# Hybrid decoder layer: projections of p in eight PSUM banks, splits queued behind evictions, first weight chunk over two queues

## Chip, cores and metric

The kernel runs on one core of one Trainium2 chip. The metric is the device time of one execution in microseconds (us); three executions before the change took 839.36, 839.38 and 839.81 us, median 839.38 us.

## The reference

One layer of a decoder trunk on 256 tokens and 2048 features, all in float32:

```python
h = rmsnorm(x, norm_mix_g)
u = h @ w_in                       # 2048 x 12288: ten fields, split by columns
...                                # short convolution branch yA, gated recurrence branch yB
m = sigmoid(ga) * (yA @ w_a_out) + sigmoid(gb) * (yB @ w_b_out)
x = x + m @ w_o
gate = sigmoid(rmsnorm(x, ple_norm_g) @ w_ple_gate)
x = x + gate * (p @ w_ple_proj)    # p: 256 tokens x 256, w_ple_proj: 256 x 2048
return rmsnorm(x, final_norm_g)
```

The product `p @ w_ple_proj` depends on no other part, and the kernel computes it first. Its result is needed only at the end.

## The kernel before

**Chunks and positions.** All weights are one stream of chunks. A chunk holds 256 rows by 512 columns of a weight matrix as a tile of 128 partitions x 1024 elements (512 KB). Its place in the stream is its position. Positions 0 to 3 are `w_ple_proj`, one chunk for each of its four column groups (kind `PP`); positions 4 to 11 are the first column group of `w_in` (kind `f`), whose left factor is x, transposed and scaled by a gain (`hT`); the rest of `w_in` and the other matrices follow. In this text w4 is the chunk of position 4.

**Three products for one.** [...] `split(pos)` makes the parts of a chunk: ScalarE writes `whi` (L124), then VectorE writes `wlo` (L125), which needs `whi`. `put_x(k)` does the same for the k-th block of 128 features of x (`xh` on ScalarE, L187, and `xl` on VectorE, L188); two blocks are needed for each of the positions 4 to 11. Each position is 12 matmuls of 128x128 by 128x512: two blocks of rows, two halves of the tokens, three products.

**The order of work.** The main loop goes through the positions. Before the matmuls of a position it splits the chunk three positions ahead (`ahead`, with the features of x that belong to it), so four split chunks exist at a time. After them it starts loads of raw chunks (three buffers of two chunks each) and advances the epilogues of earlier groups. The tile layer then orders each engine's instructions and puts in the semaphores. [...]

**PSUM.** `bank(tag)` takes a bank of 128 x 512 from one of two rings of four: `"g"` for the sums of the main loop, two banks for a group (one for each half of the tokens), and `"s"` for small products of the recurrence, which starts later; one `"s"` bank takes the ten matmuls that warm TensorE up. The four groups `PP` take two `"g"` banks each, so the third group reuses the banks of the first.

**The epilogue of `PP`.** `ep_pp` copies the two banks to SBUF on ScalarE (two `ACTIVATE` of 128x512, L643: the eviction) and two steps later sends the tile of 512 KB to DRAM (`kept`, L647), from where it is read back near the end.

**Loads at the start.** The halves of w0 (256 KB each) go over ScalarE's DMA queue (q10), all else over SyncE's (q1), in this order: p transposed (`praw`, 256 KB), w1, the small parameters, w2, then x in eight pieces of 256 KB (`xraw`, piece c for the feature blocks 2c and 2c+1) with w3, w4 and w5 in between, and all eight pieces of x before the first `kept`. Eight semaphores go round among the DMAs, so an issue may also wait for the landing of the one eight before it.

Of the kernel before, what the change touches and what calls it, by code (L numbers as in the profile page):

```python
# [11 lines left out]
AF = mybir.ActivationFunctionType  # L12
# [5 lines left out]
NT = T // P  # L18
D = 2048
KT = D // P  # L20
# [3 lines left out]
CW = 512  # L24
# [20 lines left out]
def hybrid_kernel(ctx, tc, xT, x, pT, prm, gfin, masks, w_in, w_a, w_b, w_o, w_pg, w_pp, out):  # L45
    nc = tc.nc
# [11 lines left out]
    def open_pool(name, side):  # L58
        closers[name] = ExitStack()
        pools[name] = closers[name].enter_context(  # L60
            tc.tile_pool(name=name, bufs=1, side=side, reuse_waits="tile")
        )

    def close_pool(name):
        closers.pop(name).close()
        del pools[name]
# [3 lines left out]
    state = {"tmp": "tmp1"}  # L70
# [3 lines left out]
    def nm(s):  # L74
        uid[0] += 1
        return f"{s}_{uid[0]}"

    def t4(tag="t4", bufs=None):
        bufs = bufs or {"tmp1": 8, "tmp2": 5, "tmp3": 5}[state["tmp"]]
        return pools[state["tmp"]].tile([P, 1024], F32, tag=tag, bufs=bufs, name=nm(tag))  # L80

    def bank(tag):
        return ps.tile([P, CW], F32, tag=tag, bufs=4, name=nm(tag))
# [10 lines left out]
    def load(pos):  # L94
        w, g, c = stream[pos]
        if pos // 2 not in loaded:
            raw = wp.tile([P, 2, 2 * CW], F32, tag="raw", bufs=3, name=nm("raw"))
            loaded[pos // 2] = raw
            if FIRST <= pos < FIRST + 4:
                for i in range(2):  # L100
                    nc.sync.dma_start(out=raw[:, i, :], in_=w[g, :, c + i, :])
            elif pos >= FIRST:
                nc.sync.dma_start(out=raw, in_=w[g, :, c : c + 2, :])
        return loaded[pos // 2]

    def load_first(pos, eng, pieces):

        w, g, c = stream[pos]
        for i in range(pieces):
            s = slice(i * (2 * CW // pieces), (i + 1) * (2 * CW // pieces))  # L110
            eng.dma_start(out=load(pos)[:, pos % 2, s], in_=w[g, :, c, s])  # L111

    def split(pos, halves=(0, 1)):
        w, g, c = stream[pos]
        src = load(pos)[:, pos % 2, :]

        pool, n = (pools["late"], 6) if (pos - state.get("late", len(steps))) % 10 < 6 and "late" in state else (wp, 4)
        if pos not in parts:
            parts[pos] = tuple(
                pool.tile([P, 2 * CW], F32R, tag=tag, bufs=n, name=nm(tag)) for tag in ("whi", "wlo")  # L120
            )
        hi, lo = parts[pos]
        s = slice(halves[0] * CW, (halves[-1] + 1) * CW)
        a = nc.scalar.activation(out=hi[:, s], in_=src[:, s], func=AF.Copy)  # L124
        v = nc.vector.tensor_tensor(  # L125
            out=lo[:, s], in0=src[:, s], in1=hi[:, s].bitcast(F32), op=ALU.subtract
        )
        state["splits"] = (a.ins, v.ins)
# [21 lines left out]
    TOKENS, NORM = 8, 12  # L150
    FIRST = 6

    load_first(0, nc.scalar, 2)
    praw = t4()[:, : 2 * T]
    nc.sync.dma_start(out=praw.rearrange("p (k t) -> p k t", k=2), in_=pT)
    load_first(1, nc.sync, 1)
    prm_t = const.tile([P, PRM_N], F32, name="prm_t")
    nc.sync.dma_start(out=prm_t, in_=prm)

# [480 lines left out]
    def ep_pp(j, psum):  # L640
        pw, d = t4(), dram.tile([P, 1024], F32, tag="kept", bufs=4, name=nm("kept"))
        for t in range(NT):
            nc.scalar.activation(out=pw[:, t * CW : (t + 1) * CW], in_=psum[t], func=AF.Copy)  # L643
        state["kept", j] = d
        yield
        yield
        nc.sync.dma_start(out=d, in_=pw)  # L647
# [73 lines left out]

    state["pT"] = tuple(z[:, :2, :] for z in state["yaT"])
    xraw = [t4() for _ in range(4)]
    for c in range(KT // 2):
        if c + 2 < FIRST:
            load_first(c + 2, nc.sync, 1)
        n = 2 * (c % 2)
        nc.sync.dma_start(
            out=xraw[c // 2].rearrange("p (k t) -> p k t", k=4)[:, n : n + 2, :],
            in_=xT[:, 2 * c : 2 * c + 2, :],  # L730
        )


    warm = pools["tmp1"].tile([P, 4, P], F32, tag="both", bufs=1, name="warm")
# [6 lines left out]
    def put_x(k):  # L741
        put(state["hT"], k, xraw[k // 4][:, (k % 4) * T : (k % 4 + 1) * T], gain(PRM_GMIX, k))
# [10 lines left out]
    def add_squares(q):  # L753

        tc.keep_in_program_order(nc.scalar.activation(
            out=xtok[q], in_=xtok[q], func=AF.Square, accum_out=state["ss1"][:, q : q + 1]
        ))

    def norm_of_x():
        tot = sc(NT, "tot1", 1)  # L760
        nc.vector.tensor_reduce(
            out=tot, in_=state["ss1"].rearrange("p (t h) -> p t h", t=NT),
            axis=mybir.AxisListType.X, op=ALU.add,
        )
        r = state["rstd1"] = rsqrt_of(tot, NT, D, "r1")
        state["rstd1_2"] = sc(NT, "r1s", 1)
        nc.vector.tensor_tensor(out=state["rstd1_2"], in0=r, in1=r, op=ALU.mult)
# [39 lines left out]
    def put_p(k):  # L807

        hi, lo = (z[:, k, :] for z in state["pT"])
        src = praw[:, k * T : (k + 1) * T]  # L810
        nc.vector.tensor_copy(out=hi, in_=src)
        nc.vector.tensor_tensor(out=lo, in0=src, in1=hi.bitcast(F32), op=ALU.subtract)
# [29 lines left out]
    def advance():  # L842
        for e in list(active):
            step(e)

    def finish():
        while active:
            advance()

    def ahead(pos):  # L850

        return LEAD + min(max(pos - (last_group - 20), 0) // 4, 5)
# [8 lines left out]
    psum = None  # L861
    for pos, (gi, c) in enumerate(steps[:last_group]):
        kind, j, w, g, opname = groups[gi]
        nch = w.shape[2]
        if kind == "PG" and j == 0 and c == 0:
            close_pool("m")
            open_pool("late", "left")
            state["late"] = done
        while done < min(pos + 1 + ahead(pos), len(steps)):
            if done == 0:  # L870
                for i in range(2):
                    put_p(i)
                    split(done, (i,))
            else:
                for k in range(2 * (done - 4), min(2 * (done - 4) + 2, KT)) if done >= 4 else ():
                    put_x(k)
                split(done)
            done += 1
        if pos == 4:
            begin()  # L880
        if 0 <= pos - NORM < 4:
            add_squares(pos - NORM)
        if pos == NORM + 3:
            norm_of_x()
        if pos == NORM + 4:
            active.append(ep_f(0, waiting))
            step(active[-1])
            nc.sync.dma_start(out=mask_t, in_=masks)
        if c == 0:
            psum = [bank("g") for _ in range(NT)]  # L890
        hi, lo = parts.pop(pos)
        for i in range(2):
            k = 2 * c + i
            s = slice(i * CW, (i + 1) * CW)
            for n in ((0,), (2,), (1,)) if pos == 0 and i == 0 else ((0, 1, 2),):
                for t in range(NT):
                    product(psum[t], state[opname], k, t, hi[:, s], lo[:, s], k == 0, k == 2 * nch - 1, n)


        if kind == "PG" and j == 0 and c < 2:  # L900
            advance()
        for q in range(done, min(done + AHEAD, len(steps)) if pos >= FIRST else 0):
            load(q)
        if 0 <= pos - TOKENS < 4:
            load_tokens(pos - TOKENS)
        if kind != "PG" or j or c >= 2:
            advance()
        if kind == "O" and j == 0 and c == nch - 3:
            finish()
            third_part()  # L910
        if kind == "O" and j > 0 and c == 1:
            residual(j)
        if kind == "O" and j == 2 and c == 4:
            load_gfin()
        if kind == "PG" and c == 4:
            load_projection(j)
            if j == 2:
                load_projection(3)
        if c == nch - 1:
            if kind == "f" and j == 0:  # L920

                waiting = psum
            if kind == "ga" and j == 0:
                finish()
                second_part()
            if kind == "O" and j == 0:
                state["x1T"] = operand(big, "x", KT)
            if kind == "f" and j == 0:
                continue
            active.append(epilogues[kind](j, psum))  # L930
            step(active[-1])
# [4 lines left out]
    for t, halves in ((0, (0, 1)), (1, (0,)), (1, (1,))):  # L936
        bk, n = bank("g"), CW // 2
        for c in range(nlast):
# [4 lines left out]
            for i in range(2):  # L943
                k = 2 * c + i
                s = slice(i * CW + halves[0] * n, i * CW + (halves[-1] + 1) * n)
# [83 lines left out]
```

## Time and profile before

| what | value |
|---|---|
| median of three executions | 839.38 us |
| the profiled execution, its whole time | 840.28 us |
| its span, first to last instruction | 838.5 us |
| mean granted TensorE clock | 0.993 |
| PE busy | 823.8 us (98%) |
| ScalarE (ACT) busy | 434.8 us (52%) |
| VectorE (DVE) busy | 530.5 us (63%) |
| DMA, mean over the span | 223 GB/s |

PE is TensorE's matmuls, PEld its weight loads, ACT is ScalarE, DVE VectorE, POOL GpSimd, SP SyncE. An L with a number is a line of the kernel. "idle before <-releaser" is the time for which the engine stood still before an instruction, and what ended that. In tables by stretch, PEclk is the clock that the throttle granted to TensorE, as a share of full speed, and the DMA share is the mean busy share of the 16 DMA engines. A matmul's shown duration overlaps with the next one; the distance of starts tells the pace.

### The profile page before, as it was taken

Reading aid. Unit: us, or ns where it says so; the run is one execution under the profiler, and the core shown is the slowest. Engines: PE = TensorE matmul, PEld = TensorE weight load, DVE = VectorE, ACT = ScalarE, POOL = GpSimd, SP = SyncE. Lnnn points to the kernel's source line nnn. Section 1 sums busy time; section 2 is a strip of 40 time slices with the busy share of each in tenths; the row PEclk is TensorE's granted clock in tenths of the full one; section 3 lists DMA queues with packets and bytes.
Section 4 is the critical chain, followed back from the end, with each engine's and each line's share of the span. In section 5 each row is a group of like instructions: output and inputs, shape, how many; then the busy total and the mean of one; then the engine's idle time right before and its main releaser. Section 6 shows DMA issues by size and latency. Waiting matters only on the chain.

```text
span 838.5 us, 9821 instructions
## 1 busy us (share of the span) xinstructions
PE 823.8 (98%) x3754; PEld 684.2 (82%) x3754; DVE 530.5 (63%) x602; ACT 434.8 (52%) x561; POOL 92.3 (11%) x76
## 2 busy tenths in 40 slices
PE   7999999999999999999999999999999999999995
PEld 4888888888888888888888888888888888888885
DVE  6546677787767478696745545645645556669722
ACT  7567465454565465355544444444444455566523
POOL 1000024320000025210000100100100100001210
PEclk8999999999999999999999999999999999999998
DMA  8978555545877554645755755755755687887702
GB/s 308 386 274 303 187 194 194 183 174 190 283 238 245 199 201 157 233 139 196 280 201 200 245 188 186 240 195 201 242 202 188 229 294 273 288 304 287 301 1 101
DMA packets 40656, 187.20 MB, mean 223 GB/s; under 512 B 4640, under 2 KB 13856, under 8 KB 22432
## 3 DMA queue, kind: packets, MB, share of 16 engines
q1 hardware_dynamic: 40032, 185.52, 63.7%
q10 hardware_dynamic: 576, 1.05, 0.3%
q8 instruction: 29, 0.48, 0.2%
q14 instruction: 19, 0.16, 0.1%
HBM read 172.92 MB, written 13.63 MB: 222 GB/s over the span
## 4 chain that ended last, share of the span: by engine, by line
PE 96%; issue 1%; DMA 1%; ACT 1%; DVE 0%; SPq 0%; POOLq 0%; POOL 0%; ACTq 0%
PE g L859 93%; PE s L359 1%; DMA raw<-in_w_pp 1%; PE s L468 0%; ACT whi L124 0%; PE s L480 0%; PE s L481 0%; PE s L479 0%; ACT xs L696 0%; DVE wlo L125 0%; ACT t L679 0%; SPq L111 0%; ACT xh L187 0%; DVE t L675 0%; POOLq L1024 0%
## 5 line engine op out<-in xcount | busy, mean ns | idle before, releaser
L125 DVE TENSOR_TENSOR wlo<-raw,whi 128x1024 fp32r<-128x1024 f32 (+1 forms) x293 | 361.4, 1237 | 263.4 <-ACT whi L124 261.8
L124 ACT ACTIVATE whi<-raw 128x1024 fp32r<-128x1024 f32 (+1 forms) x293 | 308.5, 1057 | 350.8 <-PE g L859 302.3
L859 PE MATMUL g<-whi,xh 128*128 128x512 f32 (+1 forms) x912 | 352.3, 387 | 0.0
L859 PE MATMUL g<-wlo,xh 128*128 128x512 f32 (+1 forms) x912 | 351.5, 385 | 0.0
L859 PE MATMUL g<-whi,xl 128*128 128x512 f32 (+1 forms) x912 | 351.4, 385 | 0.0
L859 PEld LDWEIGHTS g<-whi,xl 128*128 128x128 f32 x912 | 171.3, 188 | 34.4
L859 PEld LDWEIGHTS g<-whi,xh 128*128 128x128 f32 x912 | 171.4, 188 | 33.7
L859 PEld LDWEIGHTS g<-wlo,xh 128*128 128x128 f32 x912 | 171.4, 188 | 33.7
L859 PE MATMUL g<-wlo,mh 128*128 128x512 f32 x128 | 49.6, 389 | 0.0
L859 PE MATMUL g<-whi,ml 128*128 128x512 f32 x128 | 49.5, 389 | 0.0
L859 PE MATMUL g<-whi,mh 128*128 128x512 f32 x128 | 49.5, 389 | 0.0
L604 POOL TENSOR_TENSOR t<-ga,gb 128x512 f32<-128x512 f32 x8 | 14.2, 1795 | 249.0 <-DVE gb L600 249.0
L859 PE MATMUL g<-whi,yaTh 128*128 128x512 f32 x80 | 32.3, 406 | 4.8 <-ACT t L643 4.1
L859 PE MATMUL g<-wlo,yaTh 128*128 128x512 f32 x80 | 32.1, 403 | 0.2 <-DVE wlo L125 0.2
L859 PE MATMUL g<-whi,yaTl 128*128 128x512 f32 x80 | 31.7, 398 | 0.0
L859 PEld LDWEIGHTS g<-wlo,mh 128*128 128x128 f32 x128 | 24.0, 188 | 5.0
L859 PEld LDWEIGHTS g<-whi,ml 128*128 128x128 f32 x128 | 24.0, 188 | 5.0
L859 PEld LDWEIGHTS g<-whi,mh 128*128 128x128 f32 x128 | 24.0, 188 | 4.9
L405 POOL TENSOR_TENSOR t<-b 128x512 f32<-128x512 f32 x10 | 20.9, 2086 | 65.1 <-DVE b L309 33.6
L387 POOL TENSOR_TENSOR X<-t,kT 128x256 f32<-128x256 f32 x12 | 14.1, 1175 | 105.1 <-ACT t L401 63.4
L859 PE MATMUL g<-whi,ybTh 128*128 128x512 f32 x64 | 24.9, 389 | 0.0
L859 PE MATMUL g<-wlo,ybTh 128*128 128x512 f32 x64 | 24.9, 389 | 0.0
(142 smaller groups left out, 539.9 us busy)
## 6 DMA issues: line engine op xcount, KB each, us to landing
raw<-in_w_in SPq DMA_DIRECT2D x93, 1024.0 KB, 4.8
raw<-in_w_o SPq DMA_DIRECT2D x16, 1024.0 KB, 6.7
raw<-in_w_pg SPq DMA_DIRECT2D x16, 1024.0 KB, 5.0
turn<-t SPq DMA_DIRECT2D x72, 128.0 KB, 2.6
t<-turn SPq DMA_DIRECT2D x18, 512.0 KB, 5.3
raw<-in_w_a SPq DMA_DIRECT2D x8, 1024.0 KB, 5.0
raw<-in_w_b SPq DMA_DIRECT2D x8, 1024.0 KB, 5.0
raw<-in_w_in SPq DMA_DIRECT2D x6, 512.0 KB, 6.5
```

Of the source, the lines that this page charges most:

```text
L124: a = nc.scalar.activation(out=hi[:, s], in_=src[:, s], func=AF.Copy)
L125: v = nc.vector.tensor_tensor(out=lo[:, s], in0=src[:, s], in1=hi[:, s].bitcast(F32), op=ALU.subtract)
L359: nc.tensor.matmul(bk[:, s], X[:, 0, h, :], X[:, 1, h, :], start=True, stop=True)
L387: eng.tensor_tensor(out=xv[:, w, :, :, half, :], in0=ev[:, :, blk, :, half, :], in1=src[:, :, blk, :, half, :], op=ALU.mult,)
L405: nc.gpsimd.tensor_tensor(out=er, in0=br, in1=ref, op=ALU.subtract)
L604: nc.gpsimd.tensor_tensor(out=spread(m, t), in0=blocks(ga[:, s]), in1=blocks(gb[:, s]), op=ALU.add)
L859: nc.tensor.matmul(psum, a, b, start=first and n == 0, stop=last and n == 2)
```

## The change

Five edits:

- The `PP` groups of j = 2 and 3 take their banks from the ring `"s"`.
- `ep_pp` records its eviction, and at positions 1 to 4 everything that the loop splits (`put_x` and `split`) is queued on ScalarE behind the last recorded eviction.
- The pieces 4 to 7 of x are no longer issued at the start but at the positions 2 to 5, one each, between the sending of the `kept` tiles.
- The first half of w0 goes over ScalarE's queue, the second over SyncE's, ahead of w1. The load of p stands before both.
- The helper `load_first` takes a list of queues.

```diff
-    def load_first(pos, eng, pieces):
+    def load_first(pos, queues):
 
         w, g, c = stream[pos]
-        for i in range(pieces):
-            s = slice(i * (2 * CW // pieces), (i + 1) * (2 * CW // pieces))
-            eng.dma_start(out=load(pos)[:, pos % 2, s], in_=w[g, :, c, s])
+        n = 2 * CW // len(queues)
+        for i, eng in enumerate(queues):
+            eng.dma_start(out=load(pos)[:, pos % 2, i * n : (i + 1) * n], in_=w[g, :, c, i * n : (i + 1) * n])
...
-    load_first(0, nc.scalar, 2)
     praw = t4()[:, : 2 * T]
     nc.sync.dma_start(out=praw.rearrange("p (k t) -> p k t", k=2), in_=pT)
-    load_first(1, nc.sync, 1)
+    load_first(0, (nc.scalar, nc.sync))
+    load_first(1, (nc.sync,))
...
-            nc.scalar.activation(out=pw[:, t * CW : (t + 1) * CW], in_=psum[t], func=AF.Copy)
+            state["evicted"] = nc.scalar.activation(
+                out=pw[:, t * CW : (t + 1) * CW], in_=psum[t], func=AF.Copy
+            ).ins
...
-    for c in range(KT // 2):
-        if c + 2 < FIRST:
-            load_first(c + 2, nc.sync, 1)
+
+    def load_x(c):
         n = 2 * (c % 2)
         nc.sync.dma_start(
             out=xraw[c // 2].rearrange("p (k t) -> p k t", k=4)[:, n : n + 2, :],
             in_=xT[:, 2 * c : 2 * c + 2, :],
         )
+
+    for c in range(4):
+        load_first(c + 2, (nc.sync,))
+        load_x(c)
...
+        order = ExitStack()
+        if 1 <= pos <= 4:
+
+            order.enter_context(tc.issue_after(state["evicted"]))
         while done < min(pos + 1 + ahead(pos), len(steps)):
...
+        order.close()
+        if 2 <= pos < 6:
+            load_x(pos + 2)
...
-            psum = [bank("g") for _ in range(NT)]
+            psum = [bank("s" if kind == "PP" and j > 1 else "g") for _ in range(NT)]
```

In the built programs the first instructions stand in this order (E0 is the eviction of the group at position 0, both halves; S a split; x2,3 the two feature blocks of x; K0 the sending of a `kept` tile; X a piece of x):

| | before | after |
|---|---|---|
| ScalarE | S0a S0b S1 S2 x0,1 S3 x2,3 S4 x4,5 S5 E0 E1 x6..12 E2a x13 E2b x14 S6 E3a x15 E3b S7 S8 S9 | S0a S0b S1 S2 S3 E0 x0,1 S4 E1 x2,3 S5 E2 x4,5 x8,9 S6 E3 x6,7 S7 x10,11 x12,13 S8 S9 x14,15 |
| SyncE | p w1 prm w2 X0 w3 X1 w4 X2 w5 X3 X4 X5 X6 X7 K0 w6 w7 K1 K2 w8 w9 K3 w10/11 | p w0b w1 prm w2 X0 w3 X1 w4 X2 w5 X3 X4 K0 w6 w7 X5 K1 X6 K2 w8 w9 X7 K3 w10/11 |

Further on, the orders of all engines differ by a few swaps of neighbours only.

## Prediction

> **What bounds the kernel now.** I read the page first. TensorE fills the span:
>
> ```profile
> span 838.5 us, 9821 instructions
> PE 823.8 (98%) x3754; PEld 684.2 (82%) x3754; DVE 530.5 (63%) x602; ACT 434.8 (52%) x561; POOL 92.3 (11%) x76
> PE 96%; issue 1%; DMA 1%; ACT 1%; DVE 0%; SPq 0%; POOLq 0%; POOL 0%; ACTq 0%
> ```
>
> So only time in which PE stands still or runs below its clock can be gained. The timeline of PE has one long gap, at the third projection group:
>
> ```profile
> 11.86 0.39 PE L859 MATMUL g<-whi,yaTl 128*128 128x512 f32 x1
> 16.37 0.80 PE L859 MATMUL g<-whi,yaTh 128*128 128x512 f32 x1 [4.12 <-ACT t L643]
> ```
>
> PE waits 4.12 us for the eviction that frees a "g" bank. The table by stretch shows what follows:
>
> ```profile
> 12.25:14.31 2.06, 0.00 (x0) 0.00 (x0) 1.69 (x4) 1.53 (x4) 0.00 (x0) 1.00 1.03 411
> 14.31:16.37 2.06, 0.00 (x0) 0.00 (x1) 2.06 (x4) 1.97 (x4) 0.00 (x0) 0.50 1.06 398
> 16.37:21.14 4.77, 4.77 (x11) 3.80 (x12) 3.59 (x8) 4.71 (x12) 0.00 (x0) 0.50 0.89 259
> 24.17:60.00 35.83, 35.83 (x160) 29.67 (x159) 18.47 (x25) 20.50 (x28) 0.77 (x2) 1.00 0.90 344
> ```
>
> The seventh number is PEclk. The clock fell to 0.50 at 14.31, 2.06 us after the last matmul, and stayed there to 21.14: 4.77 us of matmuls at half speed, 2.4 us lost. From 21.14 on PE never stops; a position takes 2.72 us (12 starts 0.227 apart): position 4 starts at 24.17, position 10 at 40.49. ScalarE's timeline says why the eviction is late:
>
> ```profile
> 10.43 1.06 ACT L124 ACTIVATE whi<-raw 128x1024 fp32r<-128x1024 f32 x1 [0.34 <-DMA raw<-in_w_pp]
> 12.82 1.06 ACT L124 ACTIVATE whi<-raw 128x1024 fp32r<-128x1024 f32 x1 [0.53 <-DVE wlo L125]
> 14.78 1.06 ACT L124 ACTIVATE whi<-raw 128x1024 fp32r<-128x1024 f32 x1
> 15.74 2.04 ACT L643 ACTIVATE t<-g 128x512 f32<-128x512 f32 x4
> ```
>
> The sums of position 0 were ready at 9.4, but S4 and S5 stand ahead of the eviction, and S5 waits for w5, which lands at 14.67 (a landing here is an issue's start plus its time to landing: 6.95 + 7.7). S4's wait is put down to VectorE, but w4 lands in the same moment, at 12.72, and is what S4 needs. The DMA by stretch (PEclk, DMA share, GB/s):
>
> ```profile
> 11.50:17.00 5.50, 0.76 1.02 394
> 17.00:17.70 0.70, 0.50 0.27 100
> 19.10:22.50 3.40, 0.70 0.93 231
> 28.40:34.00 5.60, 1.00 1.03 426
> ```
>
> The queue is full until 17.0, empties because the first `kept` is issued only at 16.83, and runs at 231 GB/s for 3.4 us behind that write. This decides below.
>
> **The change, part by part.** *Banks.* Positions 2 and 3 no longer wait for an eviction. Position 4 reuses position 0's banks. No work is added.
>
> *Second half of w0 on SyncE's queue.* Now w1 (issued 1.18, landing after 5.2) shares the engines with the second half, which lands at 6.56. Standing alone ahead of w1, its 256 KB take 0.66 us at 400 GB/s behind the first half (4.53): 5.2. The bytes up to w1 are the same, so w1 lands near 6.5. SyncE has one issue more, 0.42 us, in front of w1, prm, w2, X0 and w3; w1's issue is followed by 5 us of transfer, so that is hidden. Position 0 ends near 8.0, not 9.4. Position 1 then waits for w1: S1 6.55 to 7.6, its `wlo` (1.23) to 8.87, and ten matmuls after that: 11.15. Position 2 (`wlo` at 10.2, as w2 lands at 7.9) runs to 13.9, position 3 (S3 at 10.43, `wlo` 12.75) to 16.6. Position 4 could start at 16.6 instead of 24.17: 7.6 us, namely the 4.12, the 2.4 and 1.0 at the start.
>
> *Splits behind evictions.* ScalarE's round per position is an eviction (four took 2.04, so 2 x 0.51), two features (seven took 2.91, 2 x 0.42) and a split (next start 0.97 later): 2.83 us, against PE's 2.72. From S3 at 10.43: E0 11.4, x0,1 12.4, S4 13.3 to 14.3, E1, x2,3, S5 16.1 to 17.2, E2 17.1, x4,5 and x8,9 to 19.8, S6 19.8 or when w6 is there. The sums that E0 to E3 wait for are ready at 8.0, 11.2, 13.9 and 16.6, always earlier than ScalarE comes to them, so what queues behind an eviction (features and split, VectorE behind these) pays its 1.0 us and no wait. S4's `wlo` ends at 15.5 and S5's at 18.4; PE needs them at 16.8 and 19.5. The cover is 1.1 us; without it the excess is a stall of PE.
>
> *Moved pieces of x.* K0 is issued once E0 is done, at 12.5 instead of 16.83; w6 and w7 follow, then X5 (waits for w4, 12.72), K1 at 15.2, X6, K2 at 17.9, w8, w9, X7. At each of these times transfers that land 4 us later and more are pending, so the queue doesn't empty. Who waits: X5 to X7 are needed for positions 9 to 11, near 30 us and later; they land before 31.
>
> *What is late next.* PE comes 7.6 us earlier, the loads do not. Now w6 lands at 22.48, w8 at 28.63 and w10/11 at 33.86:
>
> ```profile
> 25.61 7.08 SPq L103 DMA_DIRECT2D raw<-in_w_in x3
> raw<-in_w_in SPq DMA_DIRECT2D x1, 1024.0 KB, 8.2
> ```
>
> The bytes ahead of w10/11 are the same, so all I take off is the gap of 0.65 us. w10/11: 33.2. With three pieces of x no longer ahead of w6 (0.66 each) it lands at 19.85, w8 (one piece, X7, passes behind it) at 27.3. Position 6 could start at 22.0; `wlo` of w6 is done at 22.2, after two matmuls with `whi`, so there is no stall. Position 8 could start at 27.5; S8 ends at 28.4 and `wlo` at 29.7, so it ends at 29.7 + 10 x 0.227 = 32.0 instead of 30.2: 1.75 us lost. Position 9 to 34.7. Position 10: S10 34.3, `wlo` 35.6, 0.45 us lost; it ends at 37.9 instead of 43.2. From there the loads gain on PE (a position needs 512 KB in 2.72 us, 193 GB/s), as position 12's, landing 2.5 us behind w10/11, show: 35.7, needed at 40.6.
>
> Sum: 7.6 - 1.75 - 0.45 = 5.3 us (rounded), and all of it stays, since PE had no gap after 21.14. The profiled execution took 840.28 (span 838.5), which becomes 835.0. The median is 0.9 lower: **834.1 us**.
>
> *The unknown cost: loads between writes.* The trace shows kept writes in two kinds of company. w6 behind the first took 2.67 us instead of 1.31 (22.48 - 19.81); the two behind w7 cost 0.2 to 0.4 each, and 1.31 to 1.28 is what w9 and the last took. From X4's landing (16.02) to w10/11 6.03 MB move; at the 405 GB/s of 12 to 16 us that is 14.9, to 30.9; before it took 17.2 without the gap. So four writes cost 2.3 us in all. From below: nothing. From above: the first's rate behind each of the four, 3.4 x (1 - 231/405) = 1.46 each, 5.8. I keep the measured sum, since it is the same bytes in nearly the same order.
>
> **Rivals.** *No stall:* the slow stretch came from the burst after an empty queue and does not return. Then w8 lands near 25 and w10/11 at 30.9, and PE never waits: 7.6 us, 831.8. For it: around and behind the fourth write the queue ran at 426 GB/s. Against: the stretch from 9.0 to 11.5 ran at 316 GB/s with no write near it.
>
> *The clock falls again:* between 27.5 and 29.7 PE would stand still for 1.7 us in two pieces. Before, an idle 2.06 us brought 0.50, while the gaps of 0.3 and 0.35 before 7.3 did not. The clock's edges lie 3.41 us or multiples apart (4.07, 14.31, 21.14); half speed for one such step costs 1.7 us, of which position 10's wait takes up 0.45: 4.0 gained, 835.4. [...]
>
> *Each write costs what the first did:* w10/11 lands at 36.7, position 10's first `wlo` matmul comes at 39.1 instead of 40.94: 1.8 gained, 837.5.
>
> *Slower:* the same mechanism at a higher price. The change separates the writes, so each is followed by loads, and PE has lost the 7.6 us of slack in which these loads came in. It decides from 1.9 us per write (7.6/4). At twice the price of the first, 2.9, w10/11 lands at 42.6 and PE starts on its `wlo` at 45.0: 4.1 lost, 843.5. For it: 3.4 us at 231 GB/s. Against: no row shows a write that cost more than 1.5.
>
> That the change doesn't do what it says is excluded by the built order: the third and fourth group write "s" banks, and no split stands ahead of an eviction.
>
> **How the numbers follow.** The forecast has 0.55, no stall 0.17, the clock 0.15, costly writes 0.08, slower 0.05. A measurement can tell 0.2% (1.7 us). Costly writes lie on that border: 0.03 go to faster, 0.05 to the same. Faster 0.90, same 0.05, slower 0.05. The range takes in the first three and the near part of the fourth: 831.6 to 837.0.
>
> **What would show it.** PE's gap at the third group gone, PEclk 1.00 from 4 us on; position 4 at 16.6; E0 at 11.4; the first `kept` issued near 12.5; `ACT whi <- DMA raw` as the wait that ends last near 28 and 33; position 10 ending near 37.9. Wrong would be: a PEclk of 0.50 after 28 us, position 4 late because of ScalarE, or a w10/11 landing before 32 or after 35.

## The result and the profile after

The changed kernel takes 834.41 us (median of four executions, 833.91 to 835.07) against 839.42 us before: 5.0 us less, a ratio of 0.994 with a 95% interval of 0.9923 to 0.9957. Five more executions taken beside the experiments lie between 833.30 and 834.63, median 833.58. The forecast was 834.1 us. The profiled execution took 834.50 us, 5.78 less than the profiled one before.

The page of the changed kernel, first lines:

```profile
span 832.7 us, 9822 instructions
...
PE 821.6 (99%) x3754; PEld 682.6 (82%) x3754; DVE 530.0 (64%) x602; ACT 433.0 (52%) x561; POOL 92.4 (11%) x76
```

The table by stretch, over the times in which PE stood still or ran at half clock before, and one stretch at position 10 (columns: PE, PEld, DVE, ACT, POOL busy, PEclk, DMA share, GB/s):

```profile
12.25:14.31 2.06, 2.06 (x11) 1.71 (x10) 1.54 (x3) 2.06 (x5) 0.00 (x0) 1.00 1.02 407
14.31:16.37 2.06, 2.06 (x11) 1.71 (x10) 1.83 (x3) 2.06 (x6) 0.00 (x0) 1.00 1.04 419
16.37:21.14 4.77, 4.77 (x23) 3.95 (x22) 3.70 (x7) 4.77 (x10) 0.00 (x0) 1.00 0.94 312
...
33.68:35.03 1.35, 0.74 (x3) 0.30 (x3) 1.28 (x2) 0.99 (x2) 0.00 (x0) 1.00 1.01 413
```

PE is busy throughout the old gap, at PEclk 1.00, and makes 23 matmuls from 16.37 to 21.14 where it made 11. ScalarE's timeline has the evictions behind single splits, and its longest later wait is for a load:

```profile
10.59 1.06 ACT L124 ACTIVATE whi<-raw 128x1024 fp32r<-128x1024 f32 x1 [1.16 <-DMA raw<-in_w_pp]
11.55 1.07 ACT L643 ACTIVATE t<-g 128x512 f32<-128x512 f32 x2
...
14.26 1.08 ACT L643 ACTIVATE t<-g 128x512 f32<-128x512 f32 x2
...
32.66 2.01 ACT L124 ACTIVATE whi<-raw 128x1024 fp32r<-128x1024 f32 x2 [2.52 <-DMA raw<-in_w_in]
```

The last of these begins with S10, waiting 2.52 us for w10/11, which lands at 32.55 (landings here are an issue's start plus its time to landing; in both profiles every DMA of SyncE's queue lands in the order of issue, 278 before and 279 after). PE's timeline shows who pays for it (the products of a position are matmuls of `whi` with `xh`, `whi` with `xl` and `wlo` with `xh`):

```profile
33.29 0.39 PE L864 MATMUL g<-whi,xl 128*128 128x512 f32 x1
33.77 0.73 PE L864 MATMUL g<-whi,xh 128*128 128x512 f32 x2
35.03 0.50 PE L864 MATMUL g<-wlo,xh 128*128 128x512 f32 x1 [0.53 <-DVE wlo L125]
```

At full pace the matmul of 35.03 would have started at 33.97 (33.29 + 3 x 0.227): 1.06 us are lost here. It is the only wait of PE after position 0 that the profile names in this execution. Before, the third matmul of position 10 started at 40.94:

```profile
40.94 0.39 PE L859 MATMUL g<-whi,xl 128*128 128x512 f32 x1
```

Now it starts 5.91 us earlier, and the span is 5.8 us shorter. So the first 35 us hold the whole gain.

### The profile page after: what moved, and what is told of

Its sections match the earlier page's. It is cut to its first block, busy times and chain, and to the rows that moved or that the text cites. A ratio compares the mean times of both kernels' runs of the same rounds, so it can differ in the third digit from the quotient of the medians.

```text
span 832.7 us, 9822 instructions
## 1 busy us (share of the span) xinstructions
PE 821.6 (99%) x3754; PEld 682.6 (82%) x3754; DVE 530.0 (64%) x602; ACT 433.0 (52%) x561; POOL 92.4 (11%) x76
## 4 chain that ended last, share of the span: by engine, by line
PE 93%; DMA 2%; ACT 2%; issue 2%; SPq 0%; DVE 0%; POOLq 0%; POOL 0%; ACTq 0%
PE g L864 91%; PE s L359 1%; DMA raw<-in_w_in 1%; DMA raw<-in_w_pp 1%; ACT t L643 0%; ACT whi L124 0%; PE s L468 0%; ACT xh L187 0%; PE s L481 0%; PE s L480 0%; PE s L479 0%; SPq L111 0%; ACT xs L698 0%; DVE wlo L125 0%; ACT t L681 0%
## 5 line engine op out<-in xcount | busy, mean ns | idle before, releaser
L864 PE MATMUL g<-whi,yaTh 128*128 128x512 f32 x72 | 27.8, 391 | 0.8 <-ACT whi L124 0.8
L864 PE MATMUL g<-wlo,yaTh 128*128 128x512 f32 x72 | 28.2, 394 | 0.0
L864 PE MATMUL g<-whi,yaTl 128*128 128x512 f32 x72 | 27.9, 389 | 0.0
```

The source lines that it names most:

```text
L864: nc.tensor.matmul(psum, a, b, start=first and n == 0, stop=last and n == 2)
```

## Experiments

The theory behind the forecast, called L (loads): the wait for the eviction and the low clock cost 6.5 us; the change frees them, and what then sets the end is the landing of the loads up to w10/11. Rivals: B (the banks are what brings the gain) and O (the order on ScalarE and SyncE is). C is the part of the theory on the share of the clock. "Beside" gives the median of executions of the kernel before that were taken together with the run.

From the start of position 12 to its last matmul PE takes 783.8 us in all thirteen profiles of this study, to within 0.01 us. So whatever makes them differ happens in positions 0 to 11, or in the 8.76 to 8.88 us behind the last matmul (9.27 in one run, named below).

**The banks alone**

```diff
-            psum = [bank("g") for _ in range(NT)]
+            psum = [bank("s" if kind == "PP" and j > 1 else "g") for _ in range(NT)]
```

> The kernel before with one edit: the third and fourth projection group take "s" banks. The order of ScalarE and of the loads stays that of before. Theory L (loads): once PE does not stand still at the third group, the end is set by the landing of w10/11 and, with the old order, of w6 and w8. PE gap of 4.1 us gone, clock 1.00 throughout, position 4 starts near 17.5, w10/11 lands near 33.9 as before, PE waits at positions 6, 8 and 10, position 10 ends near 38.6: 839.4 - 4.6 = 834.8 us, within 0.8 us of the whole change. Theory O (order): the evictions still stand behind S4 and S5 and the first kept is issued at 16.8, so most of the gain needs the order of ScalarE and SyncE: at most 2 us gained, 837.4 or more.

Measured: 836.39 us (835.71 to 836.60, five executions) beside 839.58 before, 3.2 us less; the profiled execution, the fastest of the five, took 835.71, 4.6 less than the profiled one before. Two timelines of this run, ScalarE's and PE's:

```profile
15.44 2.04 ACT L643 ACTIVATE t<-g 128x512 f32<-128x512 f32 x4
17.34 1.11 ACT L643 ACTIVATE t<-s 128x512 f32<-128x512 f32 x2
...
22.77 1.06 ACT L124 ACTIVATE whi<-raw 128x1024 fp32r<-128x1024 f32 x1 [0.75 <-DMA raw<-in_w_in]
```

```profile
23.88 0.73 PE L859 MATMUL g<-whi,xh 128*128 128x512 f32 x2 [0.65 <-ACT whi L124]
25.14 0.50 PE L859 MATMUL g<-wlo,xh 128*128 128x512 f32 x1 [0.52 <-DVE wlo L125]
```

The evictions are as late as before, but no matmul waits for them; position 4 starts at 17.63. Instead PE waits at position 6 for w6, which lands at 22.7, because the first `kept` (issued at 16.53) and w6 behind it are late. Position 10 starts at 35.71 instead of 40.49. The median lies between the theories: L's 834.8 is missed by 1.6 us, and O's 837.4 by 1.0; only the profiles differ by L's 4.6. Of the three waits that L named, the one at position 6 came and cost 1.76 us, the one at position 10 cost 0.2, and position 8 had none. So L is right that a load decides, and O that the late release costs. The banks alone leave 2 to 2.8 us of the gain out (834.41 and 833.58 for the whole change).

**The order alone**

```diff
-            nc.scalar.activation(out=pw[:, t * CW : (t + 1) * CW], in_=psum[t], func=AF.Copy)
+            state["evicted"] = nc.scalar.activation(
+                out=pw[:, t * CW : (t + 1) * CW], in_=psum[t], func=AF.Copy
+            ).ins
...
+        order = ExitStack()
+        if 1 <= pos <= 4:
+            order.enter_context(tc.issue_after(state["evicted"]))
         while done < min(pos + 1 + ahead(pos), len(steps)):
...
+        order.close()
```

> The kernel before with one edit: splits and features at positions 1 to 4 queued behind the last eviction. Banks, halves and pieces of x as before. Theory L: E0 starts near 11.4, the first kept is issued near 12.5, PE waits under 0.3 us at the third group, position 4 starts at 17.6 as w0's second half is late, w10/11 lands at 31.8 to 32.6: 834.0 us (+-0.4). Theory B (the banks bring more than the 3.2 us that they brought alone only when the rest is added, and the order alone cannot replace them): 836.4 us or more.

Measured: 834.10 us (834.03 to 834.87) beside 839.62. ScalarE's timeline, and PE's at the third group:

```profile
9.99 1.06 ACT L124 ACTIVATE whi<-raw 128x1024 fp32r<-128x1024 f32 x1 [0.81 <-DMA raw<-in_w_pp]
10.96 1.07 ACT L643 ACTIVATE t<-g 128x512 f32<-128x512 f32 x2
```

```profile
11.98 0.39 PE L861 MATMUL g<-whi,yaTl 128*128 128x512 f32 x1
12.21 0.39 PE L861 MATMUL g<-whi,yaTh 128*128 128x512 f32 x1
```

E0 ends at 12.03, before PE has finished position 1, so on four "g" banks PE has no gap at the third group. The first `kept` is issued at 12.36 and w10/11 lands at 31.52, 0.3 us before what L expected. One edit gives 5.5 us, what the whole change gives to within its spread. The pieces of x were not moved alone; with the banks and the halves of w0 they add nothing clear to this edit.

**The change without the banks**

```diff
-            psum = [bank("s" if kind == "PP" and j > 1 else "g") for _ in range(NT)]
+            psum = [bank("g") for _ in range(NT)]
```

> The changed kernel with all projection groups on "g" banks. Theory L: E0 starts at 11.55 as in the changed kernel, so PE waits at the third group only until 12.2 and once more briefly at the fourth group and at position 4, 0.5 us in all; the slack of 1.06 us ahead of position 10 takes that up and the time stays that of the changed kernel, 834.4 us (+-0.3). Theory B (the banks bring the gain): without them the wait for the eviction comes back with the low clock, 838 us or more.

Measured: 833.73 us (833.58 to 833.84) beside 839.58, no slower than the whole change, and 0.4 us below L's range. PE's timeline at the third group and at position 10:

```profile
11.07 0.39 PE L864 MATMUL g<-whi,yaTl 128*128 128x512 f32 x1
11.98 0.50 PE L864 MATMUL g<-whi,yaTh 128*128 128x512 f32 x1 [0.52 <-ACT t L643]
...
33.90 0.61 PE L864 MATMUL g<-whi,xh 128*128 128x512 f32 x2
34.35 0.42 PE L864 MATMUL g<-wlo,xh 128*128 128x512 f32 x1
```

The wait for the eviction is back, at 0.52 us instead of 4.12, and the clock stays at 1.00. Position 10 has no wait here: w10/11 landed at 31.8. L had the time stay because a wait at position 10 would take the lost time up; instead the loads came earlier. B falls: banks and order are two ways out of the same wait, and the order also brings the loads forward.

**w10 and w11 as two loads, and the halves of w0**

```diff
-            if FIRST <= pos < FIRST + 4:
+            if FIRST <= pos < FIRST + 6:
```

> The changed kernel with w10 and w11 loaded by two DMAs of 512 KB instead of one of 1 MB. Theory L: w10 lands near 31.3 instead of 32.55, its low part is ready at 33.6, before PE comes to it at 33.97; the wait at position 10 (1.06 us in all) goes and the time falls to 833.3 us. Rival S (the wait at position 10 moves on to the next load): w12/13 lands near 35 and is needed at 39, so a gain under 0.3 us would mean that something else is late there; 834.1 or more.

Measured: 833.04 us (832.90 to 833.86, four executions) beside 839.58, the lowest median of the study; the nine executions of the changed kernel have a median of 833.91. PE's timeline at position 10:

```profile
33.15 0.62 PE L864 MATMUL g<-whi,xh 128*128 128x512 f32 x2
33.60 0.39 PE L864 MATMUL g<-wlo,xh 128*128 128x512 f32 x1
```

w10 lands at 30.24, w11 at 31.51, and the wait is gone; the next load doesn't take its place. With that edit in, the halves of w0 were put back on one queue:

```diff
-    load_first(0, (nc.scalar, nc.sync))
+    load_first(0, (nc.scalar, nc.scalar))
```

> The kernel with w10 and w11 as two DMAs, and both halves of w0 over ScalarE's queue again. Theory L: the early second half lets PE start position 1 about 1 us earlier; in the changed kernel that gain is spent on the wait for w10/11, and it counts here, where this wait is gone: 0.8 to 1.0 us slower than with w10 alone and the halves over two queues, 834.2 us. Rival: the halves never mattered, because w1 or w2 sets the pace of the first positions: no difference, 833.3 us.

Measured: 833.83 us (833.74 to 834.06), 0.8 more. In the profile the second half of w0 lands at 6.58 instead of 5.17 and position 4 starts at 17.61 instead of 16.75. So the second queue brings PE 0.86 us at position 4, and this reaches the end where nothing later waits for a load.

**The same without the banks**

```diff
-            if FIRST <= pos < FIRST + 4:
+            if FIRST <= pos < FIRST + 6:
...
-            psum = [bank("s" if kind == "PP" and j > 1 else "g") for _ in range(NT)]
+            psum = [bank("g") for _ in range(NT)]
```

> The changed kernel with w10 and w11 as two DMAs and all projection groups on "g" banks. Theory L: neither the banks nor the 1 MB load matter then: PE waits 0.5 us for evictions early and up to 0.3 us for w9, 833.1 us (+-0.4). Theory B: the banks are worth something once the load is split, as their 0.5 us is no longer taken up by a wait: 833.5 us or more.

Measured: 833.51 us (833.30 to 834.17) beside 840.12. That lies where both theories end. In the profile position 4 starts 0.49 us later than with the banks. The clock rose at 6.47 us, with them at 3.90 (from 3 to 5 us six matmuls keep PE busy for all 2.00 us, with the banks seven for 1.84), but of the time that this costs at position 0 only 0.13 us are left at the end of position 1. The third group starts at 11.65, where 11.44 was due; this wait and the slower matmuls behind it make the other 0.36 us. So the profile speaks for B, but with medians 0.47 us apart and spreads of 0.9 it stays open what the banks are worth with w10 alone.

**The `kept` tiles later**

```diff
         state["kept", j] = d
-        yield
-        yield
+        for _ in range(10 - j):
+            yield
```

> The changed kernel with the four kept tiles sent some 8 positions later, behind the loads of tokens. Theory L: 2 MB less ahead of w10/11, which lands near 27.5; PE does not wait after the first positions: 833.0 to 833.4 us, as with w10 alone. Rival: the four writes now stand ahead of the loads for positions 16 and more, which then come late: 834.4 us or more.

Measured: 833.59 us (833.12 to 835.89; four of five up to 833.74). The first `kept` is issued at 33.26, w10/11 lands at 26.92 and PE has no wait that the profile names after position 0. L holds on the wait; its 833.0 to 833.4 us is missed by 0.2. In the profile PE is as early as with w10 alone (last matmul at 822.49 and 822.38), but what follows takes 9.27 us, 0.4 more than there; the cause stays open. The load of w10/11 itself, issued at 18.28, landed 4.0 us after the landing before it (22.88) with no write near it.

**The changed kernel once more**

> The changed kernel once more, beside the runs of this call, with another profile. Theory L: what separates its executions is when the first loads and w10/11 land: 833.6 to 835.1 us; in the profile the wait of PE at position 10 is as long as w10/11's landing is later than 31.7. Rival: the time hangs on something else, and a profile with an earlier landing is no shorter.

Measured: 833.58 us (833.30 to 834.63); the profiled execution is the longest of the five. Its first loads came earlier than in the first profile (second half of w0 at 5.21, there at 5.60) and position 4 started at 16.76, but w10/11 landed at 32.69. PE's timeline:

```profile
33.90 0.74 PE L864 MATMUL g<-whi,xh 128*128 128x512 f32 x2 [0.26 <-ACT whi L124]
35.16 0.50 PE L864 MATMUL g<-wlo,xh 128*128 128x512 f32 x1 [0.52 <-DVE wlo L125]
```

The matmul of 35.16 could have come at 33.53 (16.76 + 6 x 2.72 + 0.45): 1.63 us lost. Of these 0.39 are lost at position 8, where PE comes before the `wlo` of w8, 0.42 at the first matmul of position 10 and 0.81 at the third. The start was 0.4 us better than in the first profile and the end the same: the landing of w10/11 decides, as L has it. The expectation's 31.7 was 0.2 us too late: in both profiles the time lost at position 10 is the landing less 31.5 (32.55 - 1.06, 32.69 - 1.23).

**The share of the clock**

The gap before was filled with matmuls that nothing needs; the result of the layer is not touched.

```diff
+FILL = 18
...
+            if pos == 2:
+                fill = carry[:, :256].bitcast(mybir.dt.bfloat16)
+                for _ in range(FILL):
+                    nc.tensor.matmul(wb, fill[:, :P], fill, start=True, stop=True)
             psum = [bank("g") for _ in range(NT)]
```

> The kernel before with 18 more matmuls of bf16 (128x512, of constants, into an idle "s" bank, whose result nothing reads) between the second and the third projection group, where PE stands still for 4.1 us. They take 18 x 0.216 = 3.9 us, so PE comes to the third group at the same 16.4. Theory C (2.4 of the 7.6 us were the low clock): PEclk stays 1.00 and the 11 matmuls after 16.37 run at full speed: 2.3 us gained, 837.1. Rival: the loads, w6 at 22.5, take it all back: 839.4.

Measured: 837.91 us (837.71 to 838.08, nine executions) beside 839.62: 1.7 us less, 0.8 above the 837.1 expected. In the profile the clock stays up:

```profile
12.20:15.70 3.50, 3.49 (x17) 1.58 (x17) 3.50 (x7) 3.32 (x6) 0.00 (x0) 1.00 1.04 403
15.70:21.60 5.90, 5.86 (x26) 4.79 (x26) 3.49 (x8) 5.51 (x14) 0.00 (x0) 1.00 0.93 265
```

Position 4 starts at 21.63, 2.54 us before that of the first profile, and the profiled execution is 2.55 us shorter. Of this 0.39 us are not the clock's: w5 landed earlier (14.13, there 14.67), and the third group started at 15.98 instead of 16.37. The medians differ by 1.7 only. So the profile before may have lost more to the clock than most executions do; the kernel before was profiled twice more, as it stands.

> The kernel before, one more profile. In the other profiles the first rise of the clock comes anywhere from 3.9 to 5.9 us, so its grid of 3.41 us lies differently in each execution. Theory C: in the kernel before, the fall and the rise around the gap move with this grid; matmuls run at half speed from 16.4 for 1.4 to 4.8 us, which makes 0.7 to 2.4 us of loss, and spans of 836.8 to 838.5. Rival: the loss is always 2.4 us and the spread of 839.1 to 841.4 among the executions before comes from elsewhere.

> The same look once more: another place of the grid, with the span longer by half of the time that matmuls spend at the low clock.

Measured: 839.52 and 839.63 us, spans 837.7 and 837.9. The first of them by stretch:

```profile
12.31:16.20 3.89, 0.00 (x1) 0.00 (x1) 3.48 (x7) 3.45 (x6) 0.00 (x0) 1.00 1.04 403
16.20:17.26 1.06, 1.06 (x5) 0.88 (x6) 0.72 (x1) 1.06 (x3) 0.00 (x0) 1.00 0.65 240
17.26:20.67 3.41, 3.41 (x10) 2.64 (x9) 2.64 (x7) 3.41 (x9) 0.00 (x0) 0.50 0.93 270
```

Here the clock falls only at 17.26, when PE has been busy again for 1.06 us, and stays low for 3.41 us instead of 6.83: 1.7 us of matmul time lost instead of 2.4. Position 4 starts at 23.39 (23.54 in the second) instead of 24.17. The mean granted clock of each execution sorts the kernel before in the same way: of the 13 beside the filler, the six at 0.993 took 840.22 to 841.35 us, the seven at 0.994 or 0.995 took 839.11 to 839.62. The first profile was one of the longer kind.

## Why the prediction was right, and where it was not

| step | forecast | measured, first and second profile |
|---|---|---|
| second half of w0 lands | 5.2 | 5.60, 5.21 |
| E0 starts | 11.4 | 11.55, 11.63 |
| first `kept` issued | 12.5 | 12.65, 12.73 |
| position 4 starts | 16.6 | 17.17, 16.76 |
| w8 lands | 27.3 | 25.92, 25.84 |
| position 8 starts, position 9 | 27.5, 32.0 | 28.05, 30.80; 27.64, 30.75 |
| w10/11 lands | 33.2 | 32.55, 32.69 |
| position 10, first `wlo` matmul | 35.6 | 35.03, 35.16 |
| gain by profiles | 5.3 | 5.78, 5.65 |

*The gap and the clock.* Right in both profiles: the profiles name no wait of PE from position 1 to the start of position 8, and PEclk is 1.00. That the banks take the wait away is true, but not needed: the order alone does it. The prediction named the banks as the edit that frees PE and gave the order only the role of not being late.

*ScalarE's round.* E0, E1 and E2 started within 0.25 us of the times forecast. The round was sized too long: from E0 to E1 and on to E2 it took 2.71 and 2.70 us, not 2.83, as an instruction starts before the shown end of the one ahead of it (x0,1 at 12.51, 0.96 us after E0, which is shown with 1.07). So ScalarE kept up with PE's 2.72. No eviction waited for PE.

*The stall at position 8.* This step failed: 1.75 us were put there, and 0.03 and 0.39 us were measured. w8 landed 1.4 us earlier than worked out, and w6 already did (18.44, not 19.85), as the first `kept` and w6 followed the pieces of x at a higher rate than the 231 GB/s carried over from before. The changed kernel's stretches (PEclk, DMA share, GB/s):

```profile
15.90:18.50 2.60, 1.00 0.98 357
18.50:21.60 3.10, 1.00 0.93 303
```

*The landing of w10/11.* 0.5 to 0.6 us earlier than forecast. From X4 (15.82) to w10/11 the loads took 16.7 us, 1.8 more than the 14.9 worked out without any cost, where 2.3 were laid on the four writes. But the time was lost at other places: at w7 and X5, and 0.94 of it at w9, which landed 2.25 us behind w8 instead of 1.31, beside a packet that is no write (last section). So the size of this term came out nearly and its reason is not shown: that is luck. What was underrated on one side (the start, by 0.2 to 0.6 us) and overrated on the other (position 8) met in the wait at position 10, which takes up what comes early. That is why the sum was better than its terms.

*The base.* The sum was made against a profile of the longer kind, 840.28, in which the clock cost 2.4 us; a typical execution before lost 1.7. Applied to the medians the gain should have been some 0.7 us less than by the profiles; measured are 5.0 and, with the second set, 6.0 (839.62 - 833.58). The spread of the changed kernel, 1.8 us, is larger than this point.

*Rivals.* No second fall of the clock came: the waits near 34 us add up to 0.6 and 0.8 us of standing still, where the fall in the first profile before came after 2.06 us, and PEclk stays 1.00 in the changed kernel's profile until the last matmul has ended. "Each write costs what the first did" and "slower" are refuted: w10/11 landed at 32.55 and 32.69, not at 36.7 or 42.6. With the writes at the same places, in the run without banks, w6 landed 1.26 us behind the first `kept` and w7 1.27 us behind w6, and with the `kept` tiles later a 1 MB load landed 4.0 us behind the one before it with no write near it. "No stall" is what some executions come close to: the run without banks had w10/11 at 31.8 and no wait for a load, but position 4 started at 17.56, not at 16.6.

## What to carry to other kernels

Where the last writer of a buffer has long finished and its reader waits, look at what stands ahead of the release on the releasing engine: reordering that one engine gave 5.5 us here, four more banks alone 3.2, because the order also moved the DMA queue that waits for the release (first `kept` issued at 12.36 and 16.53). Once a large wait is gone, list the loads in their landing order against the new, earlier times of need: the next limit was a 1 MB load of which only half was needed at first, and with it cut in two the median fell by another 0.9 us (four executions against nine). And make a sum of a microsecond against more than one profile: the clock was low for 6.83 us around the gap in one profile of the kernel before and for 3.41 us in another, and these executions took 840.28 and 839.52 us.

## What the runs showed of the hardware

**Where the clock's edges lay.** In the first profile before, the granted clock rises at 4.07 us, where the warming matmuls go from 0.427 us apart to 0.217, falls at 14.31, rises at 21.14 and falls again at 833.51, behind the last matmul. In the first profile after, it rises at 3.91 and falls at 826.52, again behind the last matmul. The stretches between these edges, 10.24, 6.83 and 812.37 us in the one and 822.61 us in the other, are 3, 2, 238 and 241 times 3.413. In the second profile before, the low clock lasted 3.41 us (17.26 to 20.67).

PE had stood still for 2.06 us when the clock fell at 14.31 (12.25 to 14.31). In the second profile before it stood still from 12.31 to 16.20, 3.89 us, and the fall came 1.06 us after it had begun again. Behind the last matmul the fall came after 3.51 us (830.00 to 833.51) and, in the changed kernel, after 2.30 (824.22 to 826.52). No fall came with the gaps of 0.31 and 0.35 us before 7.3 in the first profile before, nor with 0.79 us (4.85 to 5.63) and 0.53 us (34.50 to 35.03) in the changed kernel. What a gap between 0.79 and 2.06 us brings, and why the edges lie where they do, is not shown by these readings.

**A packet of the instruction queue beside a late load.** In the changed kernel's DMA queues from 25.4 to 26.5 us (packets, MB, share) a single packet of another queue stands among the loads:

```profile
q1 hardware_dynamic: 163, 0.42, 96.9%
q8 instruction: 1, 0.02, 5.6%
```

It starts at 25.47, holds 16384 bytes and took 0.99 us (5.6% of the time of 16 engines over these 1.1 us). w9 landed at 28.17, 2.25 us behind w8, in the profile before 1.28 us behind it (29.91 and 28.63), although the stretch moved 426 GB/s:

```profile
25.92:28.17 2.25, 1.00 1.07 426
```

The loads behind it did not catch up: X7, the last `kept` and w10/11 landed 0.66, 1.28 and 2.44 us apart, so that w10/11 was late too. In the profile before, such a packet starts at 30.38 and took 0.90 us; w10/11, the next to land after the write at 31.19, came 2.67 us behind it. At w7's late landing in the changed kernel (18.44 to 20.30) no such packet is near, and the rate was 229 GB/s. So the packet stands beside one late load; that it is the cause is not shown, as no run here moves it alone.
